# The end of a two-layer decoder trunk: the last six down tiles in three token ranges of 256, 128 and 128 columns instead of two of 256

## The chip, the cores and the metric

The kernel runs on one core of one Trainium2 chip. The metric is the device time of one execution in microseconds (us), and lower is better. A profile is one execution recorded by the hardware profiler; its span runs from the first to the last instruction of the program, and the execution's own time is a little longer.

The engines are named as in the profile: PE is TensorE's matmuls, PEld its weight loads, DVE is VectorE, ACT is ScalarE, POOL is GpSimd, and SP is SyncE, which here only issues DMAs. L196 means line 196 of the kernel.

## What is computed

The reference is a two-layer decoder with 512 tokens and 16 learned meta tokens ahead of them (528 columns), a width of 1024 and a hidden width of 4096. Each layer has a mixer (attention beside a short convolution) and an MLP. Only the end of the second layer matters here:

```python
for l in range(DEPTH):
    ...
    h = h + rmsnorm(y @ w_out[l], mix_post_g[l])
    a = rmsnorm(h, mlp_pre_g[l])
    f = jnp.square(jax.nn.relu(a @ w_up[l])) @ w_down[l]
    h = h + rmsnorm(f, mlp_post_g[l])
return h[:, N_META:]
```

`rmsnorm` multiplies each token's column by the inverse root of the mean of its 1024 squares, and by a gain for each of the 1024 features. So no output of a token can be finished before all 1024 features of `f` are there for that token; tokens do not depend on one another at this point.

## The kernel before

All activations lie with features on the 128 partitions and tokens along the free dimension. A tensor of 1024 features is `[128, 8, 528]`: eight groups k of 128 features. The tokens are cut into two ranges, `RA` = columns 0 to 272 and `RB` = 272 to 528; in the second layer, where the meta tokens are not needed any more, the first is `XA` = 16 to 272. Both are then 256 wide.

Every product is made from operands split into a high and a low part. `mm3` (L195) issues three matmuls for each k: high weights by high activations (L196), high weights by low activations (L197) and low weights by high activations (L198). One output tile, 128 features by one token range, takes 8 x 3 = 24 matmuls that add up in one PSUM bank. Each matmul has a weight load of its own. `mms` (L204) issues such a tile, with hooks that run after a given k; `gemm` (L217) is one tile and its evacuation.

The MLP (`mlp`, L984) works through the hidden width in four chunks. In each, eight up tiles make a chunk of `f`, and eight down tiles m = 0 to 7 add its product to `z`. In the last chunk of a layer, down tiles 0 and 1 are made over all columns at once (512 of them in the second layer). For tiles 2 to 7 the six weight tiles are kept, and the six are first made for the first range (L1014, L1015) and then, in `boundary` (L476), for the second.

The evacuation of a last-chunk tile is `z_evac` (L501): VectorE adds the PSUM bank to `z` (L510), ScalarE squares the sum (L279) and VectorE adds the square to the accumulator `acc` (L280, both in `add_sq`). In the second layer ScalarE then multiplies `z` by the gain (L519). For the very last tile, m = 7 over `RB`, the square is kept by itself (L513, `last_sq`) and not added.

The norm is class `Post` (L305). `start` (L312) sums `acc` over the partitions with a matmul by ones (`meansq`, L231: L235, and L237 for a square that was kept by itself; these are plain float32, and each shows as two passes), and `chain` (L240) makes the scale for each token: three ScalarE steps (L245 to L247) and two VectorE steps (L248, L249). `step` (L318) then does one group k: VectorE multiplies `z` by the scale (L324) and adds it to `h` (L327), and at the end of the program SP issues the store (L343). `steps(i)` is two groups. `finish` (L345) does `start` and all eight groups at once, two groups to an instruction (L354, L355, 128 partitions by 2 x 256), with a store per pair that SP and ScalarE's queue issue in turn (L356).

In `boundary` the order around the end is written out by hand. The first range's `start` is a hook after the last k of the second range's first tile; its steps 0 to 3 follow the evacuations of the second range's tiles 1 to 4. After the six tiles, the program's end is `pB.finish()` for the second range. Instructions of an engine run in the order in which the scheduler put them at build time; it follows this order but may exchange independent instructions of one engine.

In short, the end of the program before the change is:

1. six tiles for `XA` (144 matmuls of 256 columns);
2. six tiles for `RB` (144 matmuls of 256 columns), with the norm of `XA` and its eight stores beside them;
3. the last evacuation, the norm of `RB` over 256 columns, and its four stores.

Of the kernel before, what the change touches and what calls it, by code (L numbers as in the profile page):

```python
# [11 lines left out]
ALU = mybir.AluOpType  # L12

P = 128
D = 1024
KT = D // P
NM = 16
# [10 lines left out]
NEG = -1.0e30  # L28
RA = (0, 272)
RB = (272, 528)  # L30
XA = (16, 272)

G_PRE, G_ATT, G_CONV, G_POST, G_MPRE, G_MPOST, G_CW, G_N = 0, 8, 12, 16, 24, 32, 40, 52
# [3 lines left out]
def trunk_kernel(ctx, tc, xT, gains, sinkb, sinkm, rope, masks, maskm, ident_in, w_in, w_out, w_up, w_down, outT):  # L37
    nc = tc.nc
    ACT, DVE, POOL, PE = nc.scalar, nc.vector, nc.gpsimd, nc.tensor
# [8 lines left out]
    def bank():  # L48
        return pp.tile([P, 512], F32, tag="ps", name="ps")
# [4 lines left out]
    h = cp.tile([P, KT, L], F32, name="h")  # L54
    z = cp.tile([P, KT, L], F32, name="z")
# [139 lines left out]
    def mm3(ps, whi, wlo, ahi, alo, first, last, onto=False):  # L195
        PE.matmul(ps, whi, ahi, start=first, stop=False, skip_group_check=onto)  # L196
        PE.matmul(ps, whi, alo, start=False, stop=False, skip_group_check=onto)  # L197
        PE.matmul(ps, wlo, ahi, start=False, stop=last, skip_group_check=onto)  # L198
# [5 lines left out]
    def mms(items, act, hooks={}):  # L204


        banks = [bank() for _ in items]
        items = [(prepared[w], r, ev) for w, r, ev in items]
        for k in range(KT):
            ahi, alo = act(k)  # L210
            for (w, (t0, t1), _), ps in zip(items, banks):
                mm3(ps[:, :t1 - t0], w[0][:, k, :], w[1][:, k, :], ahi[:, t0:t1], alo[:, t0:t1], k == 0, k == KT - 1)
            if k in hooks:
                hooks[k]()
        return [lambda ev=ev, ps=ps, n=t1 - t0: ev(ps[:, :n]) for (_, (t0, t1), ev), ps in zip(items, banks)]
# [35 lines left out]
    def utile():  # L251
        return tp.tile([P, L + 2], F32, tag="u", name="u", bufs=2)
# [52 lines left out]
    class Post:  # L305
# [39 lines left out]
        def finish(self):  # L345

            t0, t1 = self.r
            n = t1 - t0
            self.start()
            both = self.s.unsqueeze(1).to_broadcast([P, 2, n])  # L350
            for k in range(0, KT, 2):
                t = utile()[:, :2 * n].rearrange("p (k t) -> p k t", k=2)
                hk = h[:, k:k + 2, t0:t1]
                DVE.tensor_tensor(t, z[:, k:k + 2, t0:t1], both, ALU.mult)  # L354
                DVE.tensor_tensor(hk, hk, t, ALU.add)  # L355
                (nc.sync, nc.scalar)[k // 2 % 2].dma_start(  # L356
                    outT.rearrange("(k p) t -> p k t", p=P)[:, k:k + 2, t0 - NM:t1 - NM], hk)

        def flush(self):
            if self.late:  # L360
# [9 lines left out]
    class Start(Post):  # L370
# [27 lines left out]
        def steps(self, i):  # L398
            super().steps(i)
            if self.r == RB:  # L400
                self.sums(i)
# [14 lines left out]
    def first_tiles(act, pB, rA, rB, nxt):  # L416


        items, tables, pcap, norm = nxt
        w = wtiles(NA)  # L420
        iA, iB = items(w, 0), items(w, 1)
        evs = []

        def rstd_a():
            pre_rstd(rA, norm)
            tables(0)

        initial = isinstance(pB, Start)
        at = (2, 4) if initial else (3, 5)
        groups = [(i,) for i in range(NA)] if initial else [(0, 1, 2), (3,), (4,)]  # L430
        steps = iter(range(4))
        for group in groups:
            i = group[0]
            hooks = {}
            if i == 0:
                hooks = {1 if initial else 4: pB.start}
            if i == at[0]:
                hooks = {at[1]: rstd_a}
            if not initial:
                evs += mms([iA[j] for j in group], act, hooks)  # L440
            elif i == 0:
                evs += mms(iA[:2], act)
            elif i >= 2:
                evs += mms([iA[i]], act, hooks)
            for n in (0, 1)[:1 if initial else 2]:
                m = next(steps, None)
                if m is not None:
                    pB.steps(m)

            ready = [evs] if initial else [evs[:3]] if i == at[0] else [[ev] for ev in evs]  # L450
            if i >= at[0]:
                for run in ready:
                    waiting = pend[:]
                    pend.clear()
                    for ev in run:
                        ev()
                    for f in waiting:
                        f()
                evs = [] if initial else evs[3:] if i == at[0] else []
        cap[0] = pcap  # L460
        evs = mms(iB[:3], act)
        pre_rstd(rB, norm)
        tables(1)
        flush()
        for ev in evs:
            ev()
            tile_done()
        for i in range(3, NA):
            waiting = pend[:]
            pend.clear()  # L470
            gemm(iB[i], act)
            for f in waiting:
                f()
            tile_done()

    def boundary(l, w, act, col, post, nxt):  # L476

        rA, rB = xrange(l)
        pA, pB = post(rA), post(rB)
        add = col == G_MPOST  # L480
        col = (l, col)
        n = len(w)
        for i in range(n):
            ev, = mms([(w[i], rB, z_evac(8 - n + i, rB, add, True, col))], act, {7: pA.start} if i == 0 else {})
            ev()
            if 0 < i < 5:
                pA.steps(i - 1)
            if 0 < i < 5 and nxt:
                with tc.issue_after(pA.dve.ins), tc.issue_after(pA.act.ins):
                    tile_done(1)  # L490
            else:
                tile_done(1)
        if nxt is None:
            pB.finish()
            return
        first_tiles(act_a, pB, rA if post(rA).nxt[0] == l else RA, rB, nxt)

    def xrange(l):
        return (RA if l == 0 else XA, RB)

    def z_evac(m, r, add, final, col):  # L501

        t0, t1 = r
        l, c = col
        g = gt[:, l, c + m:c + m + 1]

        def ev(ps):
            zz = z[:, m, t0:t1]
            if add:
                DVE.tensor_tensor(zz, zz, ps, ALU.add)  # L510
                if final and l == 1 and m == 7 and r == RB:
                    sq = tmp(t1 - t0)
                    ACT.activation(sq, zz, AF.Square)  # L513
                    last_sq.append(sq)
                elif final:
                    add_sq("z", m == 0, zz, r)
                if final:
                    if l == 1:
                        ACT.activation(zz, zz, AF.Copy, scale=g)  # L519
            elif final:  # L520
                ACT.activation(zz, ps, AF.Copy, scale=g)
                add_sq("z", m == 0, ps, r)
            else:
                ACT.activation(zz, ps, AF.Copy)
        return ev

    class Mixer:
# [8 lines left out]
        def tables(self, n):  # L536

            t0, t1 = (RA, RB)[n]
            nc.sync.dma_start(ct[:, t0:t1], rope[0][:, t0:t1])
# [33 lines left out]
        def v_evac(self, n):  # L573
            t0, t1 = (RA, RB)[n]

# [17 lines left out]
        def k_evac(self, n):  # L593
            t0, t1 = (RA, RB)[n]
            cols = slice(PAD + t0, PAD + t1)
# [388 lines left out]
    def mlp(l, nxt, first):  # L984

        xr = xrange(l)

        full = xr if l == 0 else [(xr[0][0], xr[1][1])]

        def one(evac, act):  # L990
            w = wtile()
            for r in full:
                gemm((w, r, evac(r)), act)
            tile_done()

        txs[l] = [wp.tile([P, 4, L // 2], F32R, tag="x", name="tx", bufs=3) for _ in range(3)]
        for c in range(NCH):
            if c == 0:
                for m in range(NA, 8):
                    one(lambda r: f_evac(m, r), act_a)  # L1000
            else:
                for m in range(0, 8, 2):
                    fast_pair(l, m)
            last = c == NCH - 1
            if last:
                new_acc("h")
            for m in range(2 if last else 8):
                one(lambda r: z_evac(m, r, c > 0, last, (l, G_MPOST)), act_f)
                if c == 0 and m < 4:
                    fast_sums(l, m)  # L1010
        if nxt is not None:
            clear_pad()
        w = wtiles(6)
        for m in range(6):  # L1014
            gemm((w[m], xr[0], z_evac(2 + m, xr[0], True, True, (l, G_MPOST))), act_f)  # L1015
        boundary(l, w, act_f, G_MPOST, lambda r: Post(l, G_MPOST, r, nxt), first)

    def clear_pad():
        POOL.memset(kk[:, :, :PAD].bitcast(F32), 0.0)
# [2 lines left out]
    first = [(m.items, m.tables, PCAP, "c") for m in (m0, m1)]  # L1022
# [81 lines left out]
```

## Time and profile before

| what | value |
|---|---|
| three runs | 1096.83, 1097.63 (median), 1098.42 us |
| the profiled execution's own time | 1097.51 us |
| its span | 1095.7 us |
| its granted TensorE clock, mean over the span | 0.996 |
| HBM read, written | 97.88 MB, 2.10 MB |

The views used below are these. The page's head has each engine's busy time and its share of the span. The groups have, by line, operation and shape, the count, the total and mean duration in ns, and the idle time ahead. The chain of work that ended last has, for each piece, its start in us from the span's start, its duration, engine, tile and line. The timeline has start, duration, engine, line, operation and shapes of instructions in order, with equal neighbours merged: x5 at 0.64 us means that five of them lie between the start of the first and the end of the last. In a matmul row `128*128` is the weight block, and the number behind it the streamed operand, partitions by columns. The windows have busy time and count for each engine in a stretch of time, then the granted clock (1.00 is full), the busy share of the DMA engines, and GB/s.

### The profile page before, as it was taken

What the parts mean: (1) busy time and instruction counts of PE and PEld (TensorE: products, weight loads), DVE (VectorE), ACT (ScalarE), POOL (GpSimd) and SP (SyncE); (2) the same over time, 40 slices, a digit from 0 to 9 for tenths busy, and PEclk for the clock granted to TensorE, in tenths of its full rate; (3) what the DMA queues carried; (4) which work ended last, traced back from release to release, by engine and by line L of the source; (5) the groups of instructions that cost most, each with busy time, mean ns of one, the idle gap of its engine ahead of it and who ended that gap; (6) DMA issues with size and microseconds to landing.
All of it is one profiled execution on the core that took longest, in us unless ns stands there. A gap on an engine that the chain in (4) does not pass through costs nothing.

```text
span 1095.7 us, 21642 instructions
## 1 busy us (share of the span) xinstructions
PE 1074.3 (98%) x8196; PEld 1030.8 (94%) x8196; DVE 801.3 (73%) x1895; ACT 624.6 (57%) x1510; POOL 10.8 (1%) x44
## 2 busy tenths in 40 slices
PE   8999999999999999999999999999999999999995
PEld 8999999999999999999989999999889989989995
DVE  7797886977585586586597988779947757757735
ACT  7576766665472383275365676667636625725732
POOL 2000000000000000000000000000000000000000
PEclk9999999999999999999999999999999999999998
DMA  9252122252252243144141412232422522522402
GB/s 249 64 146 59 58 78 79 77 155 59 69 152 85 59 127 110 49 124 137 26 112 39 130 58 59 78 97 82 130 72 84 154 68 79 162 68 71 143 1 77
DMA packets 206057, 102.06 MB, mean 93 GB/s; under 512 B 24000, under 2 KB 205904, under 8 KB 205952
## 3 DMA queue, kind: packets, MB, share of 16 engines
q1 hardware_dynamic: 205088, 99.89, 31.9%
q8 instruction: 64, 1.05, 0.4%
q10 hardware_dynamic: 688, 0.58, 0.2%
q14 instruction: 41, 0.34, 0.1%
q0 software_dynamic: 176, 0.21, 0.1%
HBM read 97.88 MB, written 2.10 MB: 91 GB/s over the span
## 4 chain that ended last, share of the span: by engine, by line
PE 88%; DVE 7%; ACT 1%; DMA 1%; issue 1%; SPq 1%; DVEq 0%; ACTq 0%
PE ps L196 28%; PE ps L198 28%; PE ps L197 28%; PE ps L202 1%; PE ps L684 1%; PE ps L653 1%; DVE wlo L108 1%; DVE a_lo L338 1%; DVE h L327 1%; DVE acc L280 1%; PE ps L235 1%; DMA h<-in_xT 0%; DVE t L326 0%; DMA z<-t 0%; SPq L558 0%
## 5 line engine op out<-in xcount | busy, mean ns | idle before, releaser
L197 PE MATMUL ps<-f_lo,whi 128*128 128x256 f32 (+2 forms) x1072 | 326.1, 305 | 0.0
L198 PE MATMUL ps<-f_hi,wlo 128*128 128x256 f32 (+2 forms) x1072 | 325.5, 305 | 0.0
L196 PE MATMUL ps<-f_hi,whi 128*128 128x256 f32 (+2 forms) x1072 | 322.9, 306 | 0.0
L197 PE MATMUL ps<-a_lo,whi 128*128 128x256 f32 (+3 forms) x808 | 230.2, 289 | 2.0 <-DVE a_lo L338 1.7
L196 PE MATMUL ps<-a_hi,whi 128*128 128x256 f32 (+3 forms) x808 | 227.2, 294 | 4.8 <-ACT a_hi L380 1.9
L198 PE MATMUL ps<-a_hi,wlo 128*128 128x256 f32 (+3 forms) x808 | 229.2, 288 | 0.1
L108 DVE TENSOR_TENSOR wlo<-wraw,whi 128x512 fp32r<-128x512 f32 x264 | 174.2, 688 | 51.8 <-ACT whi L107 31.5
L198 PEld LDWEIGHTS ps<-f_hi,wlo 128*128 128x128 f32 x1072 | 202.1, 189 | 9.1
L197 PEld LDWEIGHTS ps<-f_lo,whi 128*128 128x128 f32 x1072 | 201.6, 188 | 9.5
L107 ACT ACTIVATE whi<-wraw 128x512 fp32r<-128x512 f32 x264 | 153.9, 624 | 95.4 <-PE ps L197 58.4
L196 PEld LDWEIGHTS ps<-f_hi,whi 128*128 128x128 f32 x1072 | 199.5, 188 | 9.4
L196 PEld LDWEIGHTS ps<-a_hi,whi 128*128 128x128 f32 x808 | 148.1, 189 | 9.9 <-ACT a_hi L380 2.3
L197 PEld LDWEIGHTS ps<-a_lo,whi 128*128 128x128 f32 x808 | 152.6, 189 | 5.0 <-DVE a_lo L338 2.6
L198 PEld LDWEIGHTS ps<-a_hi,wlo 128*128 128x128 f32 x808 | 152.9, 189 | 1.4 <-DVE wlo L108 0.3
L510 DVE TENSOR_TENSOR z<-z,ps 128x272 f32<-128x272 f32 (+2 forms) x78 | 38.0, 487 | 99.9 <-PE ps L198 99.8
L107 ACT ACTIVATE wf<-wraw 128x512 fp32r<-128x512 f32 x96 | 59.7, 626 | 85.4 <-PE ps L197 51.8
L197 PE MATMUL ps<-a_lo,wf 128*128 128x264 f32 (+1 forms) x384 | 108.0, 282 | 0.0
L196 PE MATMUL ps<-a_hi,wf 128*128 128x264 f32 (+1 forms) x384 | 107.8, 282 | 0.0
L198 PE MATMUL ps<-a_hi,wf 128*128 128x264 f32 (+1 forms) x384 | 107.1, 283 | 0.0
L107 ACT ACTIVATE wf<-u 128x512 fp32r<-128x512 f32 x72 | 45.1, 627 | 88.4 <-PE ps L197 73.6
L108 DVE TENSOR_TENSOR wf<-wraw,wf 128x512 fp32r<-128x512 f32 x96 | 65.7, 688 | 11.5 <-ACT wf L107 10.5
L197 PEld LDWEIGHTS ps<-a_lo,wf 128*128 128x128 f32 x384 | 72.2, 188 | 0.1
(158 smaller groups left out, 1776.5 us busy)
## 6 DMA issues: line engine op xcount, KB each, us to landing
wraw<-in_w_up SPq DMA_DIRECT2D x128, 256.0 KB
wraw<-in_w_down SPq DMA_DIRECT2D x128, 256.0 KB
wraw<-in_w_in SPq DMA_DIRECT2D x56, 256.0 KB
wraw<-in_w_in SPq DMA_DIRECT2D x32, 128.0 KB
wraw<-in_w_out SPq DMA_DIRECT2D x32, 128.0 KB
wraw<-in_w_out SPq DMA_DIRECT2D x16, 256.0 KB
h<-in_xT SPq DMA_DIRECT2D x4, 272.0 KB
h<-in_xT SPq DMA_DIRECT2D x4, 256.0 KB
```

The costliest lines, as they stand in the source:

```text
L107: ACT.activation(hi, raw, AF.Copy)
L108: DVE.tensor_tensor(lo, raw, hi.bitcast(F32), ALU.subtract)
L196: PE.matmul(ps, whi, ahi, start=first, stop=False, skip_group_check=onto)
L197: PE.matmul(ps, whi, alo, start=False, stop=False, skip_group_check=onto)
L198: PE.matmul(ps, wlo, ahi, start=False, stop=last, skip_group_check=onto)
L202: PE.matmul(ps, a[n], b[n], start=first and n == 0, stop=last and n == 1)
L235: PE.matmul(ps, ones[:, which, :], acc, start=True, stop=more is None)
L280: return (eng or DVE).tensor_tensor(acc, acc, sq, ALU.add)
L327: DVE.tensor_tensor(hk, hk, t, ALU.add)
L338: DVE.scalar_tensor_tensor(a_lo[:, k, t0:t1], hk, g, a_hi[:, k, t0:t1].bitcast(F32), ALU.mult, ALU.subtract)
L510: DVE.tensor_tensor(zz, zz, ps, ALU.add)
L653: PE.matmul(outs[g], q[a][rows], k[b][rows], start=n == 0, stop=n == 2)
```

## The change

The second range is cut in two: `RE` = columns 272 to 400 and 400 to 528. A new function `ending` takes the place of `boundary` at the end of the second layer. It makes the six tiles for the first of these ranges, with the norm of `XA` beside them, then the six tiles for the second, with the norm of the first beside them, and at the end the norm of the second, which now covers 128 columns. The weight tiles are the same six, so they are used for three ranges. The square that is kept by itself is that of m = 7 in the last range. `finish` works in three pairs of instructions instead of four, of four, two and two groups, with a store for each. `boundary` loses its branch for the end of the program; what it does elsewhere stays.

```diff
+RE = (272, 400), (400, 528)
...
-            both = self.s.unsqueeze(1).to_broadcast([P, 2, n])
-            for k in range(0, KT, 2):
-                t = utile()[:, :2 * n].rearrange("p (k t) -> p k t", k=2)
-                hk = h[:, k:k + 2, t0:t1]
-                DVE.tensor_tensor(t, z[:, k:k + 2, t0:t1], both, ALU.mult)
+            for i, (k0, k1) in enumerate(((0, 4), (4, 6), (6, 8))):
+                all = self.s.unsqueeze(1).to_broadcast([P, k1 - k0, n])
+                t = utile()[:, :(k1 - k0) * n].rearrange("p (k t) -> p k t", k=k1 - k0)
+                hk = h[:, k0:k1, t0:t1]
+                DVE.tensor_tensor(t, z[:, k0:k1, t0:t1], all, ALU.mult)
                 DVE.tensor_tensor(hk, hk, t, ALU.add)
-                (nc.sync, nc.scalar)[k // 2 % 2].dma_start(
-                    outT.rearrange("(k p) t -> p k t", p=P)[:, k:k + 2, t0 - NM:t1 - NM], hk)
+                (nc.sync, nc.scalar)[i % 2].dma_start(
+                    outT.rearrange("(k p) t -> p k t", p=P)[:, k0:k1, t0 - NM:t1 - NM], hk)
...
-        if nxt is None:
-            pB.finish()
-            return
         first_tiles(act_a, pB, rA if post(rA).nxt[0] == l else RA, rB, nxt)
+
+    def ending(w):
+
+        col = (1, G_MPOST)
+        before = Post(1, G_MPOST, XA, None)
+        for r in RE:
+            for i in range(6):
+                ev, = mms([(w[i], r, z_evac(2 + i, r, True, True, col))], act_f, {7: before.start} if i == 0 else {})
+                ev()
+                if 0 < i < 5:
+                    before.steps(i - 1)
+            before = Post(1, G_MPOST, r, None)
+        before.finish()
...
-                if final and l == 1 and m == 7 and r == RB:
+                if final and l == 1 and m == 7 and r == RE[1]:
...
-        boundary(l, w, act_f, G_MPOST, lambda r: Post(l, G_MPOST, r, nxt), first)
+        if nxt is None:
+            ending(w)
+        else:
+            boundary(l, w, act_f, G_MPOST, lambda r: Post(l, G_MPOST, r, nxt), first)
```

More of the change, by code (lines that the diff above doesn't have):

```diff
@@ L487, in boundary @@
                 pA.steps(i - 1)
-            if 0 < i < 5 and nxt:
+            if 0 < i < 5:
                 with tc.issue_after(pA.dve.ins), tc.issue_after(pA.act.ins):
@@ L492, in boundary @@
                 tile_done(1)
-        if nxt is None:
-            pB.finish()
-            return
         first_tiles(act_a, pB, rA if post(rA).nxt[0] == l else RA, rB, nxt)
+    def ending(w):
[5 more added lines that the diff above has]
+                ev()
+                if 0 < i < 5:
+                    before.steps(i - 1)
+            before = Post(1, G_MPOST, r, None)
+        before.finish()
     def xrange(l):
```

## The prediction

> **What bounds the kernel now.** I read the head of the page first, then the chain of work that ended last.
>
> ```profile
> span 1095.7 us, 21642 instructions
> ...
> PE 1074.3 (98%) x8196; PEld 1030.8 (94%) x8196; DVE 801.3 (73%) x1895; ACT 624.6 (57%) x1510; POOL 10.8 (1%) x44
> ...
> PE 88%; DVE 7%; ACT 1%; DMA 1%; issue 1%; SPq 1%; DVEq 0%; ACTq 0%
> ```
>
> TensorE is busy for 98% of the span, and the chain runs along it for 88%. So a change is paid in TensorE time wherever TensorE streams, and only behind its last matmul do the other engines count. The edit touches both places: the last stretch of the stream, and the tail. I therefore asked for the chain of the last 13 us.
>
> ```profile
> 1083.32 0.13 PE ps L198
> 1083.45 0.02 issue
> 1083.47 0.43 DVE z L510
> ...
> 1084.40 0.71 PE ps L237 x2
> ...
> 1087.46 1.29 DVE u L354 x2
> 1088.75 1.21 DVE h L355 x2
> 1089.95 1.20 DVE u L354 x2
> 1091.16 0.60 DVE h L355
> ```
>
> The last matmul of the last tile ends at 1083.45. From there to 1087.46, 4.0 us, runs a chain in which each step waits for the one before: the evacuation (L510), a square (L513), the sum over partitions (L237), three ACT steps (L245 to L247) and two DVE steps (L248, L249), all 256 columns wide. Then VectorE does eight passes of 128x512 for the last norm, and the output goes out. The tail behind the last matmul is 1095.7 - 1083.45 = 12.25 us of the span.
>
> **The stream: twice the matmuls, each half as wide.** The six tiles over the last 256 columns are now 6 x 8 x 3 = 144 matmuls of 256 columns; with two ranges of 128 they are 288 matmuls of 128 columns, each with its own weight load: the page counts 8196 loads beside 8196 matmuls, so none is shared. The window over the stretch just ahead, six tiles of 256 columns, gives today's pace, and the chain shows the one other thing in it, the sum of a norm (L235).
>
> ```profile
> 1050.00:1065.00 15.00, 15.00 (x128) 15.00 (x128) 6.08 (x14) 6.34 (x13) 0.00 (x0) 1.00 0.00 1
> ```
> ```profile
> 1068.74 0.43 PE ps L235 x2
> ```
>
> 15.00 us / 128 is 0.117 us; the window also touches the matmul that was running at its start, so I take 0.118. The stretch costs 144 x 0.118 = 17.0 us now.
>
> What does one of 128 columns cost? No main matmul of this kernel has so few, so I looked for the nearest ones, by shape in the groups and then in the timeline around them.
>
> ```profile
> L202 PE MATMUL ps<-p,vv 128*128 128x64 f32 x4 | 0.5, 255 | 0.0
> ```
> ```profile
> L653 PE MATMUL ps<-kk,qm 64*64 64x128 f32 x6 | 0.3, 219 | 0.0
> ```
> ```profile
> L202 PEld LDWEIGHTS ps<-p,vv 128*128 128x128 f32 x132 | 19.0, 188 | 2.1 <-ACT p L283 1.4
> ```
> ```profile
> L684 PEld LDWEIGHTS ps<-ident,S 128*128 128x128 f32 x128 | 14.5, 140 | 0.8 <-issue 0.5
> ```
> ```profile
> 93.82 0.64 PEld L202 LDWEIGHTS ps<-p,vv 128*128 128x128 f32 x5
> ...
> 93.94 0.72 PE L202 MATMUL ps<-p,vv 128*128 128x64 f32 x5
> ```
>
> Read the four L202 matmuls first (the fifth in both rows is a 256-wide one behind them). Each streams only 64 columns against a full 128x128 weight block, and still its loads start (0.64 - 0.19) / 4 = 0.112 us apart.
>
> ```profile
> 71.26 0.91 PEld L684 LDWEIGHTS ps<-ident,S 128*128 128x128 f32 x8
> ```
> ```profile
> 65.14 0.34 PE L653 MATMUL ps<-kk,qm 64*64 64x128 f32 x6
> ```
>
> The transposes (L684) stream 128 columns against a full block: (0.91 - 0.14) / 7 = 0.110 us. The six L653 matmuls stream 128 columns too, but their blocks are 64 wide and go in pairs, one on each half of the rows: (0.34 - 0.22) / 2 = 0.06 us a pair. So a stream of 128 columns can go at 0.06, and what holds the others at 0.11 is the load of 128 weight columns. At 256 columns the stream (0.118) covers the load (0.11); at 128 it no longer does. I take 0.111 us, between the two full-block rows, which are the nearest; the ends are 0.109 and 0.118 (no gain at all from the halving). The stretch becomes 288 x 0.111 = 32.0 us, which is 15.0 more (14.4 to 17.0).
>
> The Trainium skill bears on this in "TensorE: Matmul & The Clock Gate", LDWEIGHTS: a load takes its columns over 1.2 GHz, 107 ns for 128, whatever the rows; and under Weight-path perf modes, the fast weight load is not for FP32. By that figure the stretch would be 30.7 us instead of 32.0. The rows above, 0.110 and 0.112, agree with it to within 5%.
>
> Added on TensorE as well: one more norm sum (L235, two passes), of 128 columns, inside the stream at the first range's end. Today's of 256 takes 0.43; two loads alone are 0.22. I take 0.25. It adds a wait: it stands on TensorE's queue behind the second range's first tile, with that range's other 120 matmuls behind it, and needs the first range's last squares added up (L510, L279, L280, about 0.9 us at these widths). The tile in between gives them 2.7 us, so the wait costs nothing; without that cover all 120 would be late by the 0.9. Together the stream ends **15.2 us later**.
>
> **What rides beside the stream.** A tile of 24 matmuls takes 24 x 0.111 = 2.7 us, against 2.8 now. VectorE and ScalarE need these prices by width:
>
> ```profile
> L324 DVE TENSOR_TENSOR t<-z,s 128x256 f32<-128x256 f32 x32 | 12.9, 422 | 0.1
> ```
> ```profile
> L355 DVE TENSOR_TENSOR h<-h,u 128x512 f32<-128x512 f32 x4 | 2.6, 686 | 0.0
> ```
> ```profile
> L283 ACT ACTIVATE p<-ps 128x512 fp32r<-128x512 f32 x32 | 17.6, 593 | 2.5 <-PE ps L684 2.3
> ```
> ```profile
> L283 ACT ACTIVATE p<-ps 128x128 fp32r<-128x128 f32 x1 | 0.3, 278 | 3.2 <-PE ps L721 3.2
> ```
> ```profile
> 1079.11 0.76 DVE L327 TENSOR_TENSOR h<-h,t 128x256 f32<-128x256 f32 x2
> ```
>
> VectorE falls by (686 - 422) / 256 = 1.03 ns a column, so 128 columns fewer save 0.13 us (0.42 to 0.29); ScalarE by (593 - 278) / 384 = 0.82, so 0.105 us. Two VectorE operations of 256 back to back take 0.76, that is 0.34 for the first. During the first range of 128, VectorE has per tile an evacuation and an addition (0.29 each) and the four 256-wide operations of the first norm (2 x 0.76): 2.1 us in 2.7. During the second range those four are 128 wide as well. Both fit, ScalarE has less, and the extra norm's chain (about 3 us) ends in the second tile, when its steps begin. Its eight stores go out on SP's queue, which holds nothing else there. These cost nothing; if VectorE fell behind, the last evacuation would start late by what it lacks.
>
> **The tail.** Between 1083.47 and 1087.46, three VectorE operations (L510, L248, L249) save 0.13 each, 0.40; four of ScalarE (L513, L245, L246, L247) 0.105 each, 0.42; the sum L237, two passes in 0.71, saves 0.11 to 0.32, say 0.21. That is 1.0 us off 4.0. The last norm's eight passes of 512 elements take until this end:
>
> ```profile
> 1091.07 1.29 DVE L355 TENSOR_TENSOR h<-h,u 128x512 f32<-128x512 f32 x2
> ```
> ```profile
> 1092.50:1094.30 1.80, 0.00 (x0) 0.00 (x0) 0.00 (x0) 0.00 (x0) 0.00 (x0) 0.50 0.84 291
> ```
>
> 1091.07 + 1.29 = 1092.36, so 4.9 us from 1087.46. The new passes are two of 512 and four of 256: 2 x 0.60 + 4 x 0.34 + 0.08 for the last one's full length = 2.6 us, 2.3 less. From 1092.36 to the span's end are 3.4 us of stores; 1.8 of them move the last two of 256 KB at 291 GB/s. The last two are now 128 KB each, but all three follow one another within about a microsecond, in rows of 512 bytes instead of 1024, which no store here shows; this end may gain 0.4 or lose 0.5, and I take 0.2 gained. The tail saves 1.0 + 2.3 + 0.2 = **3.5 us** (3.0 to 4.0).
>
> **The sum.** 15.2 - 3.5 = 11.7 us. The profiled execution took 1097.51 us, 1.8 beyond its span and 0.1 under the median of the runs shown (1097.63). 1097.51 + 11.7 = **1109.2 us**, 1.1% slower. With both sets of ends, 14.4 + 0.22 - 4.0 = +10.6 and 17.0 + 0.43 - 3.0 = +14.4: 1108.1 to 1111.9.
>
> **Rivals.** *The stream decides (faster).* If the loads overlap each other at 128 columns, a matmul costs what its columns cost.
>
> ```profile
> 1047.64 0.23 PE ps L197
> ```
>
> 512 columns go at 0.23 and 256 at 0.118, 0.44 ns a column, which leaves 0.061 at 128, as the paired L653 show. Then 288 x 0.061 = 17.6: the stream is 0.6 + 0.25 later and the tail 3.5 shorter, 2.7 us faster, 1094.8. For it speaks that a load lasts 0.19 and already overlaps the next one; against it, the four L202 loads, which had just such short streams. The place is the weight load of L196 to L198, and it decides below (17.0 + 3.5 - 0.25) / 288 = 0.070 us a matmul.
>
> *Loads and streams overlap in part.* If loads go ahead faster when many of one kind queue up (the L202 run was only four long, the transposes eight), the pace lies between 0.061 and 0.111, say 0.086: 24.8 us, 7.8 + 0.25 - 3.5 = +4.5, 1102.0. Against it stands that a run of four and one of eight gave the same 0.11. The Trainium skill gives such a figure, "TensorE: Matmul & The Clock Gate", Back-to-back issue gap: about 81 ns per matmul in a sustained stream of loads and matmuls at 128 columns. By it the time would be 1100.6; no run of matmuls here is as fast with full weight blocks.
>
> *The clock drops.* With loads deciding, the array streams for 0.061 of 0.111 us only, 55%. The granted clock has fallen once while TensorE had work:
>
> ```profile
> 3.90:7.30 3.40, 2.30 (x15) 1.68 (x13) 2.05 (x4) 2.66 (x6) 3.37 (x12) 1.00 1.02 306
> 7.30:10.70 3.40, 2.16 (x10) 1.41 (x10) 3.09 (x7) 3.23 (x9) 0.00 (x0) 1.00 1.17 317
> 10.70:14.20 3.50, 3.50 (x16) 3.50 (x17) 3.50 (x9) 3.50 (x9) 0.00 (x0) 0.51 1.10 224
> ```
>
> Behind a stretch of 3.4 us with ten matmuls it went to half, and 16 matmuls then took 3.5 us, 0.22 each instead of 0.12; behind one with 15 it did not. Ours would have 31 short ones in such a stretch and hardly a gap, so I think it unlikely. If it fell after 3.4 us, the other 28.6 would double: 1137.8.
>
> **How the numbers follow.** Load-bound as worked out: 0.77. Partial overlap: 0.08. Stream-bound: 0.08. Clock: 0.05. Something unnamed: 0.02. The prediction is the first. Its own range holds about 0.73; to reach 8 in 10 the range goes down to the partial overlap, so 1100.5 to 1112.0. About 0.2% (2.2 us) is what a measurement of this kernel can tell from no change. The stream-bound case lies at that edge, so I give faster 0.06, same 0.03, slower 0.91.
>
> **What would show it.** By shape, 288 matmuls of 128 columns with loads 0.109 to 0.118 us apart, PEld without gaps from the first range to the last tile, the last matmul about 15 us later, the evacuation-to-scale chain about 3.0 us instead of 4.0, the last norm's passes 2.6 instead of 4.9, and a granted clock of 1.00 until the end. Starts 0.06 to 0.09 apart would make the forecast wrong, and so would a clock of 0.50 inside the stretch or VectorE reaching the last evacuation late.

## The result, and the profile after

| | kernel before | changed kernel |
|---|---|---|
| median of four runs each | 1097.23 us | 1108.57 us |
| lowest to highest | 1096.52 to 1098.42 | 1107.01 to 1109.01 |
| ratio, 95% interval | | 1.0100 (1.0082 to 1.0117) |
| profiled execution: time, span | 1097.51, 1095.7 us | 1108.86, 1107.1 us |

The changed kernel is 1.0% slower, 11.3 us; forecast were 11.7. In the code after, lines from 31 on stand one further down, and those behind `boundary` eleven, so L196 to L198 are now L197 to L199, and L510 is L521.

The head of its page shows TensorE still filling the span. Its busy time grew by 14.7 us (1074.3 to 1089.0), more than the 11.4 us that the span grew by; the difference is what the tail behind it lost.

```profile
span 1107.1 us, 21991 instructions
...
PE 1089.0 (98%) x8342; PEld 1046.5 (95%) x8342; DVE 804.3 (73%) x1923; ACT 628.4 (57%) x1525; POOL 10.8 (1%) x44
```

The new matmuls appear in the groups by shape, three rows like this one of 96 each, and the windows over the two ranges of 128 columns give their pace (columns: stretch, its length, then busy time and count for PE, PEld, DVE, ACT and POOL, granted clock, DMA share, GB/s).

```profile
L199 PE MATMUL ps<-f_hi,wlo 128*128 128x128 f32 x96 | 26.5, 276 | 0.0
```
```profile
1070.00:1084.00 14.00, 14.00 (x128) 14.00 (x128) 8.84 (x29) 4.12 (x12) 0.00 (x0) 1.00 0.23 77
1086.00:1097.00 11.00, 11.00 (x101) 11.00 (x100) 5.84 (x27) 3.38 (x10) 0.00 (x0) 1.00 0.13 37
```

14.00 / 128 is 0.109 us and 11.00 / 101 the same. The counts take in the two or three that were running at a window's edge, so such a quotient is a little low here and below; from start to start the median is 0.111. Half the columns, and a matmul is 6% quicker than the 0.118 of 256. PEld is busy without a gap in both windows and the clock holds at 1.00. VectorE is at 8.84 us of 14, so it was not what held the stretch.

The chain that ended last, from the two norm sums in the stream to the end:

```profile
1068.05 0.48 PE ps L236 x2
...
1084.56 0.27 PE ps L236 x2
...
1098.07 0.13 PE ps L199
...
1098.22 0.30 DVE z L521
...
1098.54 0.32 ACT t L524
...
1098.90 0.50 PE ps L238 x2
1099.43 0.38 ACT t L246
...
1100.84 0.30 DVE s L250
1101.16 1.03 DVE u L355 x2
1102.19 0.94 DVE h L356 x2
1103.13 0.35 DVE u L355
1103.50 0.43 DVE h L356
```

From the first norm's sum to the end of the last matmul the chain took 1083.45 - 1068.74 = 14.7 us before and 1098.20 - 1068.05 = 30.15 now. The chain of single steps takes 1101.16 - 1098.22 = 2.9 us instead of 4.0, the passes of the last norm 1103.93 - 1101.16 = 2.8 instead of 4.9, and the stores behind them 3.2 instead of 3.4.

### The profile page after: what moved, and what is told of

Same layout as the page of the kernel before. It is cut to its first block, busy times and chain, and to the rows that moved or that the text cites. A ratio compares the mean times of both kernels' runs of the same rounds, so it can differ in the third digit from the quotient of the medians.

```text
span 1107.1 us, 21991 instructions
## 1 busy us (share of the span) xinstructions
PE 1089.0 (98%) x8342; PEld 1046.5 (95%) x8342; DVE 804.3 (73%) x1923; ACT 628.4 (57%) x1525; POOL 10.8 (1%) x44
## 4 chain that ended last, share of the span: by engine, by line
PE 88%; DVE 7%; DMA 1%; ACT 1%; SPq 1%; issue 1%; DVEq 0%; ACTq 0%
PE ps L197 28%; PE ps L199 28%; PE ps L198 28%; PE ps L203 1%; PE ps L695 1%; PE ps L664 1%; DVE a_lo L339 1%; DVE h L328 1%; DVE wlo L109 1%; PE ps L236 1%; DVE acc L281 1%; DMA h<-in_xT 1%; DMA wraw<-in_w_in 1%; DVE t L327 0%; DVE t L325 0%
## 5 line engine op out<-in xcount | busy, mean ns | idle before, releaser
L198 PE MATMUL ps<-f_lo,whi 128*128 128x256 f32 (+3 forms) x1120 | 338.9, 304 | 0.0
L199 PE MATMUL ps<-f_hi,wlo 128*128 128x256 f32 (+3 forms) x1120 | 338.6, 304 | 0.0
L197 PE MATMUL ps<-f_hi,whi 128*128 128x256 f32 (+3 forms) x1120 | 335.6, 305 | 0.0
L197 PE MATMUL ps<-a_hi,whi 128*128 128x256 f32 (+3 forms) x808 | 227.3, 295 | 5.3 <-ACT a_hi L381 2.2
L198 PE MATMUL ps<-a_lo,whi 128*128 128x256 f32 (+3 forms) x808 | 230.1, 289 | 1.8 <-DVE a_lo L339 1.7
L199 PE MATMUL ps<-a_hi,wlo 128*128 128x256 f32 (+3 forms) x808 | 228.9, 287 | 0.0
L199 PEld LDWEIGHTS ps<-f_hi,wlo 128*128 128x128 f32 x1120 | 211.4, 189 | 9.1
L198 PEld LDWEIGHTS ps<-f_lo,whi 128*128 128x128 f32 x1120 | 211.0, 188 | 9.6
L197 PEld LDWEIGHTS ps<-f_hi,whi 128*128 128x128 f32 x1120 | 208.9, 188 | 9.4
L197 PEld LDWEIGHTS ps<-a_hi,whi 128*128 128x128 f32 x808 | 148.3, 189 | 10.1 <-ACT a_hi L381 2.8
L198 PEld LDWEIGHTS ps<-a_lo,whi 128*128 128x128 f32 x808 | 152.6, 189 | 4.9 <-DVE a_lo L339 2.6
L199 PEld LDWEIGHTS ps<-a_hi,wlo 128*128 128x128 f32 x808 | 152.7, 189 | 1.1
L521 DVE TENSOR_TENSOR z<-z,ps 128x272 f32<-128x272 f32 (+3 forms) x84 | 38.9, 463 | 108.2 <-PE ps L199 108.0
L198 PE MATMUL ps<-a_lo,wf 128*128 128x264 f32 (+1 forms) x384 | 108.0, 282 | 0.0
L197 PE MATMUL ps<-a_hi,wf 128*128 128x264 f32 (+1 forms) x384 | 107.8, 282 | 0.0
L199 PE MATMUL ps<-a_hi,wf 128*128 128x264 f32 (+1 forms) x384 | 107.1, 283 | 0.0
L109 DVE TENSOR_TENSOR wf<-wraw,wf 128x512 fp32r<-128x512 f32 x96 | 65.6, 687 | 11.4 <-ACT wf L108 10.4
L281 DVE TENSOR_TENSOR acc<-acc,t 128x256 f32<-128x256 f32 (+2 forms) x145 | 59.6, 416 | 18.0 <-ACT t L280 17.2
```

The source lines that it names most:

```text
L109: DVE.tensor_tensor(lo, raw, hi.bitcast(F32), ALU.subtract)
L281: return (eng or DVE).tensor_tensor(acc, acc, sq, ALU.add)
```

## The experiments

The theory is the prediction's: a weight load costs by its weight columns, loads of 128 follow one another 0.11 us apart (a row of one lasts 0.19, so in the profile neighbours overlap, but they come no faster), a load runs beside the streams, and it sets the pace where the stream is shorter. Its rivals were a fixed price for every matmul with its load; a stream that is slower by the column below 256; and, from the second step on, the clock. The kernel before was run on the same chip as each experiment; its medians there, from 1096.45 to 1097.23 us, are given with the results.

**A smaller weight block.** Edit to the changed kernel, in `mms` for the two ranges of 128; the evacuation adds both halves to the same 64 features, and the other 64 of each tile get nothing:

```diff
+                    for j in range(2):
+                        c, n = slice(64 * j, 64 * j + 64), t1 - t0
+                        mm3(ps[:64, j * n:j * n + n], w[0][:, k, c], w[1][:, k, c], ahi[:, t0:t1], alo[:, t0:t1], ...)
```

> The changed kernel, but in the two ranges of 128 columns each matmul uses a weight block of 64 columns, twice as many of them (576), and only the first 64 of each tile's 128 features are evacuated; the rest is left out. Load theory (a weight load costs by its columns and sets the pace where the stream is shorter): a load of 64 columns takes about 0.057 us, the stream of 128 columns 0.061, so the pace falls to 0.057 to 0.066 us and the stretch from 32 to 33-38 us; time 1110 to 1115. Rival, a fixed cost of about 0.11 us for each load and matmul: the pace stays at 0.111 and the stretch becomes 64 us; time about 1141. Rival, the stream itself is at half rate below 256 columns: the pace also stays near 0.11 and the time near 1141.

Measured: 1110.57 us in one run (before, on the same chip: 1096.45). The windows of its ranges:

```profile
1070.00:1084.00 14.00, 14.00 (x237) 14.00 (x235) 9.25 (x32) 3.57 (x10) 0.00 (x0) 1.00 0.23 77
1086.00:1098.00 12.00, 12.00 (x204) 12.00 (x202) 6.63 (x30) 3.60 (x11) 0.00 (x0) 1.00 0.12 34
```

14.00 / 237 is 0.059 us (0.060 from start to start). The same 128 columns are streamed, and twice as many instructions are issued; only the block is half as wide, and the pace falls from 0.111 to 0.060. That rules out the fixed price, and it rules out the slow stream. What held the changed kernel was the load of 128 weight columns.

**Other widths in the stream.**

```diff
-RE = (272, 400), (400, 528)
+RE = (272, 464), (464, 528)
```

> The changed kernel with the last two ranges 192 and 64 columns wide instead of 128 and 128. Load theory: both paces stay at 0.111 us (a stream of 192 columns would take 0.09), the stretch stays at 32 us, the chain behind it and the last norm get 64 columns narrower, 0.5 + 1.2 us, and the time is about 1106.8. Rival, a stream at half rate below 256 columns: 0.167 us at 192 columns and 0.056 at 64, the same sum but two different paces. Rival, a pace by columns at full rate would have given 0.09 and 0.03.

Measured: 1117.85 us, ratio 1.0197 (1.0182 to 1.0212) to the kernel before. It is 11 us above what the load theory expected. The windows show where:

```profile
1068.00:1080.50 12.50, 12.50 (x114) 12.50 (x114) 8.69 (x27) 5.31 (x13) 0.00 (x0) 1.00 0.20 65
1081.20:1082.60 1.40, 1.40 (x16) 1.40 (x14) 0.71 (x2) 0.78 (x2) 0.00 (x0) 1.00 0.55 187
1082.60:1086.00 3.40, 3.40 (x32) 3.40 (x31) 0.55 (x3) 1.52 (x6) 0.00 (x0) 1.00 0.00 0
1086.10:1107.80 21.70, 21.70 (x103) 21.70 (x104) 6.05 (x26) 2.49 (x9) 0.00 (x0) 0.50 0.11 37
```

192 columns go at 12.50 / 114 = 0.110 us, and 64 columns at 3.40 / 31 = 0.110 as well (0.112 from start to start for both), as the theory has it. But 4.8 us into the range of 64 columns the granted clock (the third number from the right) falls to 0.50 and stays there, and from then on a matmul takes 21.70 / 103 = 0.21. About 100 matmuls that cost 0.1 more each are the missing 11 us. So the load theory gave the pace, and the rival that the prediction had put at 5%, the clock, decided the time of this kernel. It did not happen at 128 columns.

**Where the clock falls.** The next cut lies in between, 36% of streaming; the edit is `RE = (272, 432), (432, 528)`.

> The changed kernel with the last two ranges 160 and 96 columns wide. Load theory alone: the pace stays at 0.111 for both, the tail gets 0.9 us shorter, time about 1107.7. What the clock does is open: with 64 columns (a stream of 0.027 in a pace of 0.111, 24%) it fell to half, with 128 (48%) it did not; 96 columns stream 36% of the time. If it falls, the last range's pace doubles to 0.213 after 4 to 7 us, and the time is 1116 to 1119.

Measured: 1115.92 us, 1.0176 (1.0160 to 1.0193) to the kernel before, which had 1096.91. The windows:

```profile
1068.00:1081.00 13.00, 13.00 (x117) 12.95 (x116) 8.72 (x28) 5.03 (x13) 0.00 (x0) 1.00 0.19 62
1085.00:1090.00 5.00, 5.00 (x47) 5.00 (x46) 2.09 (x9) 2.23 (x7) 0.00 (x0) 1.00 0.07 20
1090.10:1103.00 12.90, 12.90 (x63) 12.90 (x62) 4.10 (x18) 1.97 (x6) 0.00 (x0) 0.50 0.12 38
```

Both widths went at 0.11 again, and the clock fell again, later (8.3 us into its last range). To see whether the narrow matmuls do it or the small share of streaming, the same ranges were run with weight blocks of 64 columns, by the edit of `half_blocks`:

> As half_blocks (weight blocks of 64 columns, twice as many matmuls, half of each tile's features left out), with the ranges of cut_160_96. The last range again streams 96 columns a matmul, but a load of 64 columns takes 0.057 us, so the array streams for 40 of about 57 ns, 70% of the time instead of 36%. If the clock goes by the share of time in which columns stream, it holds at 1.00 through the last range, 288 x 0.057 to 0.061 = 16.4 to 17.6 us, and the time is near 1115 (160 columns at 0.078: 22.5 us, so the stretch is 39 to 40 us instead of 32). Rival, it goes by the width of the matmuls: it falls to half within 4 to 9 us as in cut_160_96, and the time is above 1121.

Measured: 1114.35 us in one run (before: 1096.53).

```profile
1069.00:1086.00 17.00, 17.00 (x229) 16.92 (x228) 10.29 (x33) 5.04 (x13) 0.00 (x0) 1.00 0.15 49
1090.00:1104.00 14.00, 14.00 (x241) 14.00 (x241) 7.58 (x33) 4.25 (x13) 0.00 (x0) 1.00 0.14 42
```

With 96 columns at 14.00 / 241 = 0.058 us the clock holds to the end of the stream. (160 columns go at 17.00 / 229 = 0.074 here instead of 0.11: with the load halved, their stream sets the pace.) In both kernels PE and PEld are busy throughout, and the width is the same, so the width alone does not do it. What differs is the block and, with it, how much of the time columns stream. At 0.44 ns a column, the difference between matmuls of 512 and of 256 (0.23 and 0.118 us), 64 columns stream for 28 ns, 96 for 42 and 128 for 56. By that, columns streamed 25% and 38% of the time where the clock fell, 51% and 73% where it held (the expectations have 24, 36, 48 and 70%, with a slightly shorter column). The block alone does not do it either, since blocks of 128 held at 128 columns; nor does the number of matmuls, which was the same there. A block of 64 with as small a share as 38% was not run, so the share is the reading that fits all four, not one that is shown by itself. The Trainium skill ("TensorE: Matmul & The Clock Gate", The HAM clock gate) says that the clock drops to half after a window of about 3.4 us in which the engine is idle. Here no such window was idle by the profile, so an idle engine is not the only thing that lets the clock fall. Whether the time in which the array waits for loads counts as idle is not shown; it would fit.

**Fewer loads for the same columns.** The high weights are loaded once; the activations' two parts lie side by side in one tile, so that one matmul of 2 x 128 columns takes the place of two of 128:

```diff
-                mm3(ps[:, :t1 - t0], w[0][:, k, :], w[1][:, k, :], ahi[:, t0:t1], alo[:, t0:t1], k == 0, k == KT - 1)
+                    PE.matmul(ps[:, :2 * n], w[0][:, k, :], f_both[:, :, k, t0:t1], start=k == 0, stop=False)
+                    PE.matmul(ps[:, :n], w[1][:, k, :], ahi[:, t0:t1], start=False, stop=k == KT - 1)
```

> The changed kernel, but in the two ranges of 128 columns the high weights are loaded once for both activation parts: one matmul of 256 columns (high and low activations side by side, added up at the evacuation by a second VectorE operation) and one of 128 for the low weights. Load theory: per k 0.118 + 0.111 instead of 3 x 0.111, the stretch falls from 32 to 22 us, one more evacuation step of 0.3 us at the end, time about 1098.8. Rival, the cost lies in the streamed columns (384 for each k, as before): the stretch stays near 32 us and the time near 1108.6.

Measured: 1101.29 us, 1.0042 (1.0030 to 1.0055) to the kernel before (1096.45). A third of the loads is gone, the same 384 columns are streamed for each k, and the time falls by 7 us against the changed kernel: the load theory again. But 10 were expected. The timeline at the border between the two ranges, PE and then VectorE, shows one reason (in brackets the idle time before and who ended it):

```profile
1080.97 0.22 PE L216 MATMUL ps<-f_both,wlo 128*128 128x128 f32 x1
1082.38 0.46 PE L241 MATMUL ps<-acc,ones 128*128 128x128 f32 x2 [1.19 <-DVE acc L286]
```
```profile
1080.57 0.75 DVE L333 TENSOR_TENSOR h<-h,t 128x256 f32<-128x256 f32 x2
1081.24 0.80 DVE L527 TENSOR_TENSOR z<-z,ps 128x128 f32<-128x128 f32 x3
1081.95 0.28 DVE L286 TENSOR_TENSOR acc<-acc,t 128x128 f32<-128x128 f32 x1
```

TensorE stands for 1.2 us, because the norm sum needs the last addition to `acc`, and VectorE has that queued behind the first norm's steps and behind the second evacuation operation that this edit adds to every tile. It is the wait that the prediction priced at nothing as long as a tile lasts 2.7 us; here a tile lasts 1.8, and the cover is gone. The next run moves that `start` one tile later (`if i == 1`, the steps behind tiles 2 to 5):

> As shared_load, but the first norm's start comes after the second tile of each range instead of the first, and its steps follow tiles 2 to 5. If the 1.4 us in which TensorE stood at the border of the two ranges come from the norm sum's wait for VectorE, which has fallen behind in tiles of 1.8 us, the gap goes and the time falls by about 1.2 us, if no other run of VectorE is late in its place at the end. Rival, TensorE stood for another reason (a bank, a weight): the gap stays.

Measured: 1098.62 us, 1.0017 (1.0008 to 1.0027) to the kernel before (1096.53). On the timeline the sum now follows the stream at once:

```profile
1082.37 0.22 PE L216 MATMUL ps<-f_both,wlo 128*128 128x128 f32 x1
1082.43 0.44 PE L241 MATMUL ps<-acc,ones 128*128 128x128 f32 x2
```

The wait is gone, and with it the time is 10 us under the changed kernel, as was expected of `shared_load`. This is the fastest way of the three-range kind that was run, and it is still 2 us slower than the kernel before. By the theory it should be: the stream takes 96 x (0.118 + 0.111) = 22.0 us against 17.0, the tail gains 3.4 and loses 0.3 to the added evacuation, so 5.0 - 3.1 = 1.9. The two medians differ by 2.7 us, more than the wait of 1.2; that part stays open, since the runs of both kernels scatter by some 4 us. Part of the scatter is the clock far ahead of the change: in the slowest run of `shared_load`, which is the profiled one, it also stood at 0.50 from 592.4 to 595.8 us, where that of the kernel before had 1.00.

**Many cuts that stay wide.** Edit to the kernel before, in `mlp`:

```diff
-        full = xr if l == 0 else [(xr[0][0], xr[1][1])]
+        full = xr
```

> The kernel before, with every 512-column product of the second layer's MLP (696 matmuls) cut into two of 256, so 696 more matmuls and loads, all of them at least 256 columns wide; the ends of the ranges stay as in the kernel before. Load theory: a load of 0.111 us hides behind a stream of 0.118, so each pair costs 0.236 instead of 0.232, in all +2.8 us, about 1100. Rival, each added matmul with its load costs what the change's 144 cost, 15.2 / 144 = 0.106 us: +73 us, about 1170.

Measured: 1100.77 us, 1.0035 (1.0022 to 1.0048), so +2.4 to +5.3 us on 1096.45. The window in the MLP has 20.00 / 171 = 0.117 us a matmul.

```profile
980.00:1000.00 20.00, 20.00 (x171) 20.00 (x170) 9.24 (x17) 3.49 (x7) 0.00 (x0) 1.00 0.23 64
```

Nearly five times as many added loads as the change has (696 against 144) cost about 4 us, a quarter of the 15.3 by which the changed kernel's stream ended later. Cutting is nearly free as long as the pieces stream longer than a load.

**A cut at the point where both meet.** `RE = (16, 288), (288, 528)`; the six tiles for the first range move into `ending`, and `finish` works in four passes of two groups, as in the kernel before.

> The last six tiles in two ranges of 272 and 240 columns (16 to 288, 288 to 528) instead of 256 and 256, and a last norm of 240 columns in four passes of two groups. Load theory: 240 columns is where stream and load meet; the two ranges cost 144 x (0.125 + 0.111) = 34.1 us against 144 x 0.236 = 34.0 now, the chain and the passes behind gain 0.1 + 0.26 us, so the time is 0.3 us under the kernel before, no difference that can be measured, and the pace of the 240-column matmuls is 0.111 to 0.113. Rival, every matmul under 256 columns pays a step: 240 columns at 0.15 to 0.22, +5 to +15 us.

Measured: 1096.23 us against 1096.91 for the kernel before, ratio 0.9994 (0.9985 to 1.0003): no difference that can be told. The window over its last range gives 13.00 / 118 = 0.110 us for 240 columns (0.112 from start to start).

```profile
1070.00:1083.00 13.00, 13.00 (x118) 13.00 (x118) 9.63 (x27) 5.57 (x13) 0.00 (x0) 1.00 0.20 66
```

So there is no step at 256 columns; the pace goes down with the width until it meets the load.

**One range left out.** In `ending`, `for r in RE[1:]`.

> The changed kernel without its range of columns 272 to 400: these columns get no last-chunk product in tiles 2 to 7, no norm and no store. Half of the stretch's columns are left out of the kernel before. Load theory: 144 matmuls at 0.111 are 16.0 us against 17.0 in the kernel before, and the tail is 3.35 us shorter, so about 4.4 us under the kernel before. Rival, a cost by columns: 8.8 us instead of 17.0, so about 11.5 us under the kernel before.

Measured: 1091.32 us in one run, 5.6 under the kernel before. Its chain has the first norm's sum at 1066.81 and the end of the last matmul at 1080.65, 13.8 us against 14.7, and 8.9 us behind it against 12.25. That is 4.2 us, and 0.2 more in the first tile: the theory's 4.4. The rest lies far ahead of the change: in this execution the clock did not fall at the program's start. By the trace the first norm's sum stands 1.9 us earlier than in the kernel before, 0.2 of it for the narrower tile ahead of it.

```profile
10.70:14.20 3.50, 3.50 (x31) 3.50 (x30) 3.41 (x9) 3.38 (x9) 0.00 (x0) 1.00 1.19 251
```

In the kernel before, the same window had a clock of 0.51 and 16 matmuls instead of 31. In the stretch just ahead of it, 7.30 to 10.70 us, it had 10 matmuls, and this execution 14.

**The grouping of the last norm.** `finish` of the changed kernel in four pairs, `enumerate(((0, 2), (2, 4), (4, 6), (6, 8)))`.

> The changed kernel with the last norm in four passes of two groups (2 x 128 columns each, four stores) instead of four, two and two groups. Load theory says nothing of it; by the widths, eight passes of 0.34 us are 2.8 us against 2.8 now, so the time is the same within 0.3 us. Rival, the longer first pass and the smaller number of stores are part of what the tail gained: 0.5 to 1 us slower.

Measured: 1107.61 us, 1.0099 (1.0084 to 1.0114); the changed kernel had 1.0100. Four, two and two groups or four times two make no difference that can be told here; on the profile the passes take 2.77 us in both. What the tail gained it owes to the width.

## Why the prediction was right

Each term against the profile after:

| term | forecast | measured |
|---|---|---|
| pace at 128 columns | 0.111 us | 0.111 |
| stream with the added norm sum | +15.2 us | +15.3 (30.15 - 14.7, less 0.2 for the quicker tile ahead of it) |
| the added norm sum itself | 0.25 us | 0.27 |
| chain of steps behind the last matmul | -1.0 us | -1.05 |
| passes of the last norm | -2.3 us | -2.1 |
| stores at the end | -0.2 us | -0.2 |
| ahead of the change | 0 | -0.5, another execution |
| sum | +11.7 us | +11.4 on the span, +11.3 on the medians |

The 0.5 us ahead of the change are not the change's; without them the terms come to +11.9. That the sum is as close as 0.3 is in part luck, the terms themselves are not.

The step that carried it was to look for a row with a full weight block and a short stream. The four L202 matmuls of 64 columns were in the trace only in the first layer's meta tokens, and they gave 0.112 where their columns alone would have given 0.03. `half_blocks` shows that the reading was right for the reason given: with half the block the time of a matmul is about half, 0.060 us.

The passes took 2.77 us where the forecast had 2.6, mostly because the last addition needs the product just ahead of it and starts only when that has ended, 0.45 us after its start; the forecast priced that step at the 0.34 us of an operation that overlaps its neighbour. VectorE and ScalarE held nothing up, as worked out; `shared_load` shows how close that was, since tiles of 1.8 us with one more operation each for VectorE were enough to lose the cover.

Of the rivals, the stream as the bound and the partial overlap are out: with a full block the pace was 0.11 at 64, 96, 128, 160, 192 and 240 columns. (The Trainium skill's 81 ns at 128 columns, "TensorE: Matmul & The Clock Gate", Back-to-back issue gap, was not seen in any run: at 128 columns they have 0.111 us with a full block and 0.060 with half of one.) The clock was rightly held unlikely at 128 columns, but for too weak a reason. The prediction counted 31 matmuls in a stretch and hardly a gap; `cut_192_64` had as many and fell. What kept the change at 1% is, by the shares above, that streaming for half of the time was still enough.

## What to carry to other kernels

Before cutting a matmul's columns, find the width at which its stream meets its weight load; here that is about 240 columns for a block of 128 in float32r, and narrower pieces saved nothing more (0.11 us down to 64 columns). A shorter tail must pay for that: here 3.4 us were gained and 15.3 spent. Where the stream fills less than about half of the time, look at the granted clock too: in `cut_192_64` its fall cost 11 us, about as much as the whole change.

## What was not expected of the hardware

The clock fell to half with TensorE busy by every row, when columns streamed 25% and 38% of the time, and held at 51% and 73%. Where between 38% and 51% the border lies was not tried, and that the share decides is argued from these four. Loads of 64 weight columns came 0.058 us apart and those of 128 0.111, so the price goes by the columns of the block. And the clock does not always fall during the program's first loads: the execution of `one_range` in which it did not had its first norm's sum 1.9 us earlier (1066.81 against 1068.74), and of what is ahead of that point only one tile is changed, which accounts for 0.2.
